# A column roll on one core: the head columns in sixteen stages through one pair of buffers instead of four stages with buffers of their own

## The chip, the cores and the metric

The kernel runs on one core of one Trainium2 chip. Time is device time in microseconds of one execution of the whole program; a kernel's time is the median over its runs. The profile is of one such execution, and "span" is the time from its first to its last profiled instruction.

## The reference

```python
x = np.random.randn(8192, 8192).astype(np.float32)
shift = 100

def reference(x, shift):
    return np.roll(x, shift, axis=1)
```

Every row of 8192 floats is turned to the right by 100 places: `out[r, c] = x[r, c - 100]`, and the last 100 columns of a row come to its front. There is no arithmetic; 268 MB are read and 268 MB written.

## The kernel before

The kernel cuts each row in two. With `s = 100` the cut column is `a = 256`, and `g = a - s = 156`.

**The bulk** is columns 256 to 8191 of the output, copied from HBM to HBM (line 43). Rows are taken in 128 blocks of 64; a block is four DMAs of 16 rows each, in turn on SP's and on ACT's queue. A row of a DMA is 31,744 B, one DMA 496 KB. In the last four blocks each is cut into two of half the width. Nothing waits for the bulk and it waits for nothing.

**The heads** are columns 0 to 255 of the output, 1 KB a row, and go through SBUF on GpSimd's queue. Four consecutive rows are numbered `q = 0..3`. For rows `q = 1..3` one read (`t`, line 73) fetches 256 floats that begin 100 floats ahead of the row: these are the last 100 of the row before and the first 156 of the row itself. So `t[q - 1]` holds the front part of output row `q - 1` (its first 100 columns) and the back part of output row `q` (its other 156). Two small reads complete the set: the last 100 floats of row 3 (line 74) and the first 156 of row 0 (line 77), straight into `h`. Two copies on DVE (lines 75 and 78) put the halves from `t` into `h`, whose rows are then the finished heads, and four stores (line 82), one for each `q`, write them.

Before the change a stage is 2048 rows: 128 partitions, `J = 4` groups of four rows in each, so that a large read and a store carry 512 rows of 1 KB. There are four stages, and each has buffers of its own (`bufs=n_st`). The first loop (lines 67 to 79) issues all the reads and copies of all stages, the second loop (lines 80 to 82) all the stores.

What orders this work: GpSimd issues its DMAs one after another, in the order of the program. The framework gives these DMAs eight completion semaphores in rotation, so a DMA can't be issued before the one eight places ahead of it has landed. It also writes the waits that the data need: a copy for the reads it uses, a store for the copies and small reads that filled its rows, and, where a buffer is used again, the new writer for the last reader.

Of the kernel before, what the change touches and what calls it, by code (L numbers as in the profile page):

```python
# [1 line left out]

# [4 lines left out]


@with_exitstack
def kernel(  # L10
    ctx: ExitStack,
    tc: tile.TileContext,
    x: bass.AP,
    shift: int,
    out: bass.AP,
):
    nc = tc.nc
    n_rows, n_cols = x.shape
    s = shift % n_cols
    a = -(-s // 128) * 128  # L20
    if 0 < a <= 384 and a + 128 <= n_cols:
        a += 128
    g = a - s
    P = nc.NUM_PARTITIONS
    engines = [nc.sync, nc.scalar]
    n_chunks = 16
    rows = n_rows // n_chunks

    xm = x.rearrange("(c e j) w -> c j e w", e=16, j=4)
    om = out.rearrange("(c e j) w -> c j e w", e=16, j=4)
    if a < n_cols:
        blocks = n_rows // 64
        mid = (a + n_cols) // 256 * 128
        for c in range(blocks):
            parts = ((a, mid), (mid, n_cols)) if c >= blocks - 4 and a < mid else ((a, n_cols),)  # L40
            for j in range(4):
                for lo, hi in parts:
                    engines[j % 2].dma_start(out=om[c, j, :, lo:hi], in_=xm[c, j, :, lo - s:hi - s])
    if a == 0:
        return


    if a > 512:
        for i in range(n_chunks):
            r = slice(i * rows, (i + 1) * rows)  # L50
            nc.gpsimd.dma_start(out=out[r, :s], in_=x[r, n_cols - s:])
            if g > 0:
                nc.gpsimd.dma_start(out=out[r, s:a], in_=x[r, :g])
        return

    Q, J = 4, 4  # L60
    n_st = n_rows // (P * Q * J)
    reads = ctx.enter_context(tc.tile_pool(name="reads", bufs=n_st))
    heads = ctx.enter_context(tc.tile_pool(name="heads", bufs=n_st))
    xt = x.rearrange("(k p j q) c -> k q p j c", q=Q, j=J, p=P)
    ot = out.rearrange("(k p j q) c -> k q p j c", q=Q, j=J, p=P)
    tiles = []
    for k in range(n_st):
        t = reads.tile([P, Q - 1, J, a], x.dtype)
        h = heads.tile([P, Q, J, a], x.dtype)
        for q in range(1, Q):  # L70
            lead = bass.AP(tensor=x.tensor, offset=(k * P * J * Q + q) * n_cols - s,
                           ap=[[J * Q * n_cols, P], [Q * n_cols, J], [1, a]])
            nc.gpsimd.dma_start(out=t[:, q - 1], in_=lead)  # L73
        nc.gpsimd.dma_start(out=h[:, Q - 1, :, :s], in_=xt[k, Q - 1, :, :, n_cols - s:])  # L74
        nc.vector.tensor_copy(h[:, :Q - 1, :, :s], t[:, :, :, :s])  # L75
        if g > 0:
            nc.gpsimd.dma_start(out=h[:, 0, :, s:], in_=xt[k, 0, :, :, :g])  # L77
            nc.vector.tensor_copy(h[:, 1:, :, s:], t[:, :, :, s:])  # L78
        tiles.append(h)
    for k, h in enumerate(tiles):  # L80
        for q in range(Q):
            nc.gpsimd.dma_start(out=ot[k, q, :, :, :a], in_=h[:, q])  # L82


# [1 line left out]
_INS = ['x', 'shift']  # L86
_OUTS = [((8192, 8192), 'float32')]

_NUMBERS = {'shift': 100}


# [26 lines left out]
```

## Time and profile before

| | us |
|---|---|
| four runs | 833.5, 830.17, 828.19, 826.13 |
| median | 829.18 |
| the profiled execution | 833.5 |
| its span | 831.3 |
| DVE busy | 7.7 (8 copies) |
| POOL busy | 28.8 (40 instructions, 36 of them DMA issues) |
| first and last bulk issue | 0.7 and 824.6 |
| first and last head store issued | 183.9 and 379.2 |

How to read it: SP and ACT only issue DMAs here, and issuing is not counted as busy on them. On POOL, DMA_DIRECT2D is the issue of a DMA. The queue q0 is GpSimd's (the heads), q1 and q10 are SP's and ACT's (the bulk). The row "GB/s" gives, in 40 equal slices of the span (20.8 us each), what the DMA engines moved; a byte copied from HBM to HBM counts once there, although it is read from HBM and written to it. DVE's two copies of a stage take 0.79 us (line 75) and 1.1 to 1.3 us (line 78). The median times from issue to landing are 12.8 us for a bulk DMA of 496 KB, 5.9 to 6.0 us for those of 248 KB at the end, 97.2 us for a large head read, 95.2 and 100.3 us for the small ones, and 115.7 us for a head store.

### The profile page before, as it was taken

What the parts mean: (1) busy time and instruction counts of PE and PEld (TensorE: products, weight loads), DVE (VectorE), ACT (ScalarE), POOL (GpSimd) and SP (SyncE); (2) the same over time, 40 slices, a digit from 0 to 9 for tenths busy, and PEclk for the clock granted to TensorE, in tenths of its full rate; (3) what the DMA queues carried; (4) which work ended last, traced back from release to release, by engine and by line L of the source; (5) the groups of instructions that cost most, each with busy time, mean ns of one, the idle gap of its engine ahead of it and who ended that gap; (6) DMA issues with size and microseconds to landing.
All of it is one profiled execution on the core that took longest, in us unless ns stands there. A gap on an engine that the chain in (4) does not pass through costs nothing. (4 is left out here: it accounts for less than half of the span.)

```text
span 831.3 us, 633 instructions
## 1 busy us (share of the span) xinstructions
DVE 7.7 (1%) x8; POOL 28.8 (3%) x40
## 2 busy tenths in 40 slices
DVE  0000000000000000000000000000000000000000
POOL 3000000010010000000000000000000000000000
DMA  9999999999999999999999999999999999999998
GB/s 300 340 335 338 341 352 339 342 342 353 350 335 347 344 344 354 344 350 339 339 326 323 328 321 331 319 335 325 322 341 319 330 333 325 327 333 322 333 306 295
DMA packets 21572, 276.89 MB, mean 333 GB/s; under 512 B 9024, under 2 KB 9024, under 8 KB 13120
## 3 DMA queue, kind: packets, MB, share of 16 engines
q10 hardware_dynamic: 8448, 130.04, 46.5%
q1 hardware_dynamic: 8448, 130.04, 46.0%
q0 software_dynamic: 4672, 16.78, 6.6%
q14 instruction: 4, 0.03, 0.0%
HBM read 268.44 MB, written 268.44 MB: 646 GB/s over the span
## 5 line engine op out<-in xcount | busy, mean ns | idle before, releaser
L82 POOL DMA_DIRECT2D out_dram<-h x16 | 13.2, 825 | 199.5 <-DMA out_dram<-h 112.0
L73 POOL DMA_DIRECT2D t<-in_x_dram x12 | 9.5, 793 | 61.3 <-DMA h<-in_x_dram 32.1
L75 DVE COPY h<-t 128x1200 f32<-128x1200 f32 x4 | 3.1, 785 | 239.1 <-DMA t<-in_x_dram 239.1
L78 DVE COPY h<-t 128x1872 f32<-128x1872 f32 x4 | 4.9, 1225 | 0.0
L74 POOL DMA_DIRECT2D h<-in_x_dram x4 | 3.0, 747 | 46.0 <-DMA t<-in_x_dram 46.0
L77 POOL DMA_DIRECT2D h<-in_x_dram x4 | 3.0, 748 | 44.0 <-DMA t<-in_x_dram 44.0
L99 POOL MEMSET const-float32-0.0<- 128x1 f32 x1 | 0.1, 98 | 0.2 <-issue 0.2
L99 POOL MEMSET const-bfloat16-1.0<- 128x1 bf16 x1 | 0.1, 101 | 0.0
L99 POOL MEMSET const-uint8-127<- 128x1 uint8 x1 | 0.1, 100 | 0.0
L99 POOL MEMSET const-float32-1.0<- 128x1 f32 x1 | 0.1, 98 | 0.0
## 6 DMA issues: line engine op xcount, KB each, us to landing
out_dram<-in_x_dram SPq DMA_DIRECT2D x248, 496.0 KB, 12.8
out_dram<-in_x_dram ACTq DMA_DIRECT2D x248, 496.0 KB, 12.8
out_dram<-h POOLq DMA_DIRECT2D x16, 512.0 KB, 115.7
t<-in_x_dram POOLq DMA_DIRECT2D x12, 512.0 KB, 97.2
out_dram<-in_x_dram SPq DMA_DIRECT2D x16, 248.0 KB, 5.9
out_dram<-in_x_dram ACTq DMA_DIRECT2D x16, 248.0 KB, 6.0
h<-in_x_dram POOLq DMA_DIRECT2D x4, 312.0 KB, 95.2
h<-in_x_dram POOLq DMA_DIRECT2D x4, 200.0 KB, 100.3
```

The source lines that it names most:

```text
L73: nc.gpsimd.dma_start(out=t[:, q - 1], in_=lead)
L74: nc.gpsimd.dma_start(out=h[:, Q - 1, :, :s], in_=xt[k, Q - 1, :, :, n_cols - s:])
L75: nc.vector.tensor_copy(h[:, :Q - 1, :, :s], t[:, :, :, :s])
L77: nc.gpsimd.dma_start(out=h[:, 0, :, s:], in_=xt[k, 0, :, :, :g])
L78: nc.vector.tensor_copy(h[:, 1:, :, s:], t[:, :, :, s:])
L82: nc.gpsimd.dma_start(out=ot[k, q, :, :, :a], in_=h[:, q])
L99: nc = _bacc.Bacc("TRN2", target_bir_lowering=False, num_devices=1)
```

## The change

A stage is now 512 rows: one group of four rows in each partition, so that a large read and a store carry 128 rows of 1 KB. There are sixteen stages. Both pools have one buffer, so every stage uses the same `t` and the same `h`. The second loop is gone: a stage's four stores are issued right behind its reads and copies. The bulk is not touched.

```diff
-    Q, J = 4, 4
-    n_st = n_rows // (P * Q * J)
-    reads = ctx.enter_context(tc.tile_pool(name="reads", bufs=n_st))
-    heads = ctx.enter_context(tc.tile_pool(name="heads", bufs=n_st))
-    xt = x.rearrange("(k p j q) c -> k q p j c", q=Q, j=J, p=P)
-    ot = out.rearrange("(k p j q) c -> k q p j c", q=Q, j=J, p=P)
+    Q = 4
+    n_st = n_rows // (P * Q)
+    reads = ctx.enter_context(tc.tile_pool(name="reads", bufs=1))
+    heads = ctx.enter_context(tc.tile_pool(name="heads", bufs=1))
+    xt = x.rearrange("(k p q) c -> k p q c", q=Q, p=P)
+    ot = out.rearrange("(k p q) c -> k p q c", q=Q, p=P)
     tiles = []
     for k in range(n_st):
-        t = reads.tile([P, Q - 1, J, a], x.dtype)
-        h = heads.tile([P, Q, J, a], x.dtype)
+        t = reads.tile([P, Q - 1, a], x.dtype)
+        h = heads.tile([P, Q, a], x.dtype)
         for q in range(1, Q):
-            lead = bass.AP(tensor=x.tensor, offset=(k * P * J * Q + q) * n_cols - s,
-                           ap=[[J * Q * n_cols, P], [Q * n_cols, J], [1, a]])
+            lead = bass.AP(tensor=x.tensor, offset=(k * P * Q + q) * n_cols - s, ap=[[Q * n_cols, P], [1, a]])
             nc.gpsimd.dma_start(out=t[:, q - 1], in_=lead)
-        nc.gpsimd.dma_start(out=h[:, Q - 1, :, :s], in_=xt[k, Q - 1, :, :, n_cols - s:])
-        nc.vector.tensor_copy(h[:, :Q - 1, :, :s], t[:, :, :, :s])
+        nc.gpsimd.dma_start(out=h[:, Q - 1, :s], in_=xt[k, :, Q - 1, n_cols - s:])
+        nc.vector.tensor_copy(h[:, :Q - 1, :s], t[:, :, :s])
         if g > 0:
-            nc.gpsimd.dma_start(out=h[:, 0, :, s:], in_=xt[k, 0, :, :, :g])
-            nc.vector.tensor_copy(h[:, 1:, :, s:], t[:, :, :, s:])
-        tiles.append(h)
-    for k, h in enumerate(tiles):
+            nc.gpsimd.dma_start(out=h[:, 0, s:], in_=xt[k, :, 0, :g])
+            nc.vector.tensor_copy(h[:, 1:, s:], t[:, :, s:])
         for q in range(Q):
-            nc.gpsimd.dma_start(out=ot[k, q, :, :, :a], in_=h[:, q])
+            nc.gpsimd.dma_start(out=ot[k, :, q, :a], in_=h[:, q])
```

## The prediction

> **What bounds the kernel now.** I read the page from its slices down, then the timeline of GpSimd's queue, then the table by windows. The page first:
>
> ```profile
> DMA  9999999999999999999999999999999999999998
> GB/s 300 340 335 338 341 352 339 342 342 353 350 335 347 344 344 354 344 350 339 339 326 323 328 321 331 319 335 325 322 341 319 330 333 325 327 333 322 333 306 295
> DMA packets 21572, 276.89 MB, mean 333 GB/s; under 512 B 9024, under 2 KB 9024, under 8 KB 13120
> q10 hardware_dynamic: 8448, 130.04, 46.5%
> q1 hardware_dynamic: 8448, 130.04, 46.0%
> q0 software_dynamic: 4672, 16.78, 6.6%
> HBM read 268.44 MB, written 268.44 MB: 646 GB/s over the span
> ```
>
> The DMA engines are busy in every slice; DVE and POOL are busy for 7.7 and 28.8 us of 831.3. The end is set by the bulk on SP's and ACT's queues (q1, q10), whose last transfers are issued at 824.6 us. Heads (q0) are 16.78 of 276.89 MB. So the question is not what the head path costs, but when it ends, and what a byte costs.
>
> The issues of GpSimd's queue give the pace (start, duration, instruction, and in brackets the idle time before it and what ended it):
>
> ```profile
> 62.40 0.75 POOL L73 DMA_DIRECT2D t<-in_x_dram  x1 [5.54 <-DMA h<-in_x_dram]
> ...
> 125.30 0.75 POOL L73 DMA_DIRECT2D t<-in_x_dram  x1 [6.34 <-DMA h<-in_x_dram]
> ...
> 261.45 0.71 POOL L82 DMA_DIRECT2D out_dram<-h  x1 [8.19 <-DMA h<-in_x_dram]
> ...
> 379.16 0.71 POOL L82 DMA_DIRECT2D out_dram<-h  x1 [12.55 <-DMA out_dram<-h]
> ```
>
> Each issue waits for the landing of the DMA eight places earlier. Eight stores take (379.16 - 261.45) / 8 = 14.7 us each; a stage of five reads takes 125.30 - 62.40 = 62.9 us. The last store is issued at 379.2 and lands some 116 us later (the median of its row in the issues), at 495: heads are done 335 us before the bulk.
>
> **What a packet costs.** There are 528 + 36 = 564 DMAs, and 564 x 16 = 9024 is exactly the count under 512 B: every DMA closes with one signal on each of 16 engines. On q0 that leaves 4672 - 576 = 4096 data packets of 4096 B on average for 36 x 512 = 18,432 rows: the short rows go out packed, some 4.5 to a packet, and none is under 2 KB. A 512 KB DMA is then 8 data packets and a signal per engine, 9 turns: 14.7 / 9 = 1.63 us a turn. During the stores a 512 KB DMA every 14.7 us is 35.7 GB/s; the window 320 to 400 us moves 346, so the bulk moves 310, or 19.4 GB/s per engine, and in 1.63 us that is 31.7 KB: one bulk packet (496 KB over 16 engines is 31,744 B). So a head packet waits for one bulk packet, and a signal takes a turn like any other. The reads: 3 x 9 turns, and for the two small ones 8 data packets and 2 signals, 37 turns in 62.9 us, 1.70 us each.
>
> **The byte price.** Two lines of the table by windows (window, length, busy, clock, DMA share, GB/s) stand for storing and bulk alone:
>
> ```profile
> 320.00:400.00 80.00, 0.00 (x0) 3.57 (x5) 1.00 1.01 346
> 520.00:600.00 80.00, 0.00 (x0) 0.00 (x0) 1.00 1.00 326
> ```
>
> Bulk bytes touch HBM twice, head bytes once. Storing: 2 x 310 + 36 = 656 GB/s of HBM; bulk alone 652, and 660 in the window 680 to 760 (330 GB/s). While heads are read (80 to 160 us, 341 GB/s) a stage of 2.10 MB in 62.9 us is 33 GB/s, so 2 x 308 + 33 = 649. HBM traffic is what is nearly constant; a head byte costs its share whenever it is moved.
>
> **The change, part by part.**
>
> *Bytes and rows:* the same; no term.
>
> *DMAs:* 144 instead of 36, each of 128 rows. Issue takes POOL 0.75 us for 512 rows, so 108 more are at most 81 us, between about 0 and 0.75 each; I take the upper end. Per stage that is 9 x 0.75 = 6.8 us, and it lies beside packets in flight. There are 108 more signals per engine; a signal's record in the trace takes 9 ns, so 1 us of engine time, but each costs the head queue a turn.
>
> *Turns per stage:* three reads of 8 KB per engine, 2 data and a signal, 9 turns; the small reads of 3.2 and 5.0 KB per engine, 2 and 3 turns, 5 together; four stores, 12. At the prices above 14 x 1.70 + 12 x 1.63 = 43.4 us a stage, 694 us for 16. The first DMA of the run landed some 9 us later than its turns say (about 24 us instead of 15), so heads end near **705 us**, against 495, and still 125 us before the bulk.
>
> *New waits:* with one pair of buffers, in the built program's waits, (a) the two small reads of a stage wait for the four stores of the stage before; queued behind them on POOL are only the stores, and the three large reads have been issued ahead, 9 turns or 15 us of queued work. (b) The copies on DVE wait for the large reads and those stores, and the first stores for the copies: at most 2.1 us of copies (0.79 + 1.32 before, for four times the size) and 1.6 us for an issue behind them, under 5 turns (8.5 us) of small reads. (c) The last two stores (three in the first stage) wait for the small reads, under 6 turns of the first two stores, 9.8 us. Each handover has a cover longer than its cost, so I take 0 a stage; without covers I bound it at 3 x 4 = 12 us (copies and issue of 3.7 us at (b) taken for all three).
>
> *Old waits removed:* the eight-deep run-ahead. The trace's 16 signals of the store issued at 307.3 us arrive from 317.6 to 423.0: most engines are soon done, four lag by up to 72 turns. Now no engine can be more than about a stage ahead. The slow ones set the pace in both forms, and I count nothing.
>
> *Interleaving:* reads at 649 instead of 656 GB/s for 180 us cost 2 us now; spread over 700 us this may vanish or double. I put -4 to +5 us on it, with the start, and take +1 for the signals.
>
> **The sum** on the profiled execution: 833.5 us (span 831.3) + 0 + 1 = 834.5. That execution was the slowest of four; carried to the median 829.18, the forecast is **830 us**. A step of 1% either way, 8 us, is about what a measurement of this kernel can tell from no change.
>
> **A rule against it.** The Trainium skill, "Trainium Kernel Development and Optimization", Best Practices, asks for double buffering so that DMA and compute overlap; one pair of buffers breaks that, and whether the queue's cover replaces it no run shows yet. The skill's "DMA: Bandwidth & Descriptors", Anatomy of one DMA, gives a GpSimd DMA a fixed cost of about 2.0 us; by it, as an estimate, 108 more DMAs paid one after another would be 216 us, and heads would end near 711 us, which is no other time for the kernel. The trace's price of a signal turn, 1.63 us, is near that figure.
>
> **The rivals.**
>
> *Heads outlast the bulk (slower).* The place is the three handovers, and it decides from (826 - 10) / 16 = 51 us a stage, 7.6 us above my sum. For it: every handover waits for the slowest of 16 engines, and the engines scatter by tens of us today. Against: the covers. At 43.4 + 12 = 55 us a stage, 14.9 stages are done when the bulk ends near 828 us; the other 1.1 run alone. No row shows a lone stage; the nearest is the last bulk transfers, landing 5.9 us after issue, so three legs are 18 us, between 3 us (1 MB at 333 GB/s) and the full 55. 1.1 x 18 = 20 us: 848 us on the profiled scale, **844** on the median. Chance 0.24.
>
> *The rows are no longer packed.* If a packet held one row, a large DMA would be 9 turns, a stage 81, some 135 us; 6 stages would be done at the bulk's end, and ten at 25 us would follow: about **1060 us**. Against it: the 400 B and 624 B rows, too, went packed, since no data packet is under 2 KB. Chance 0.03.
>
> *Bulk and heads disturb each other.* Heads now pass 512 rows in 43 us where the bulk takes 52, so both work on nearly the same rows throughout; today heads ran far ahead. If the 649 GB/s of the reading phase held to 705 us instead of 180, 1.1% of 525 us, 6 us, would be lost, and above 1% with the start: **838**. Chance 0.05.
>
> *Faster.* If mixing restored 656 GB/s throughout and smoothed the start (318 GB/s in the first 40 us), 4 us would go: **825**. That is inside 1% and part of my forecast; beyond it no row has a price. A gain over 1%, 815 to 820, keeps 0.06 for engines that lag less when heads cannot pile up eight deep.
>
> **How the numbers follow.** Heads stay hidden: 0.62, with a range of its own of 823 to 836. Slower by over 1% is 0.24 + 0.03 + 0.05 = 0.32, faster 0.06. The range reaches from 822, just inside the gain, to 850, over the 844 of the first rival, and leaves out the unpacked case, part of the gain and the worse end of the handovers.
>
> **What would show it.** In the slices GB/s should lie near 335 to 345 up to about slice 34 and fall to 328 after, where now the step is at slice 20. The last head store should be issued near 685 us; stores of successive stages should be 43 us apart; the landing of a large read should fall from 97 us to 20 to 35 us. q0 should hold some 6,400 to 6,700 packets. HBM should stay at 645 GB/s. I am wrong if stages are over 51 us apart, if q0 has packets under 2 KB by the thousand, or if the bulk's own issues end later than 830 us while the heads are long done.

## The result

The changed kernel takes 831.16 us in the median of 50 runs, the kernel before 829.54 us in 79: a ratio of 1.0019, with a 95% interval of 1.0012 to 1.0026. That is 1.6 us, 0.2%, clear of the noise but within the 1% that was called no change. The forecast was 830, with a range of 822 to 850.

The profiled execution took 831.86 us (span 830.1). The same lines of its page as those shown of before:

```profile
DMA  9999999999999999999999999999999999999998
GB/s 305 346 328 332 335 346 336 343 333 337 335 340 337 338 337 346 345 333 342 342 330 343 336 342 331 336 339 339 342 337 341 334 328 320 332 327 330 321 306 295
DMA packets 23559, 276.92 MB, mean 334 GB/s; under 512 B 10752, under 2 KB 11008, under 8 KB 15104
q1 hardware_dynamic: 8448, 130.04, 45.8%
q10 hardware_dynamic: 8448, 130.04, 44.2%
q0 software_dynamic: 6656, 16.79, 8.9%
HBM read 268.44 MB, written 268.44 MB: 647 GB/s over the span
```

The DMA engines are as full as before, and HBM carries 647 GB/s over the span against 646. What has moved is the step in the row GB/s: the heads' share now lies over slices 1 to 32 of 40, where it lay over the first 20 to 24. Heads end at 673 us (the last packet of q0 in the trace) instead of 495, still 156 us before the last packet of the bulk.

The queues' shares say more. The heads' packets now take 8.9% of the time of the 16 DMA engines, where they took 6.6%, and the bulk's take 90.0% where they took 92.5%. A bulk packet of 31,744 B passed in 1448 ns on average, against 1492 in the kernel before. So the longer time of the heads on the engines did not add to the time of the kernel: the bulk's packets became shorter by about as much, which fits a limit that lies in the traffic and not in the engines' time.

The timeline of GpSimd's queue shows one stage of the steady state and the last stores (start, duration, instruction, and in brackets the idle time before it and what ended it):

```profile
615.02 1.60 POOL L72 DMA_DIRECT2D t<-in_x_dram  x3
630.78 0.53 POOL L73 DMA_DIRECT2D h<-in_x_dram  x1 [14.16 <-DMA out_dram<-h]
631.31 0.54 POOL L76 DMA_DIRECT2D h<-in_x_dram  x1
647.28 1.08 POOL L79 DMA_DIRECT2D out_dram<-h  x2 [15.43 <-DVE h L77]
653.29 1.07 POOL L79 DMA_DIRECT2D out_dram<-h  x2 [4.93 <-DMA h<-in_x_dram]
```

The three handovers can be read from the brackets: the small reads wait for the stores, the first two stores for the copies, the last two for the small reads. The copies on DVE give the spacing of stages (line 74, the second stage and the last):

```profile
67.95 0.37 DVE L74 COPY h<-t 128x300 f32<-128x300 f32 x1 [47.25 <-DMA t<-in_x_dram]
...
646.24 0.37 DVE L74 COPY h<-t 128x300 f32<-128x300 f32 x1 [39.61 <-DMA t<-in_x_dram]
```

(646.24 - 67.95) / 14 = 41.3 us a stage, where 43.4 was forecast and 51 was the limit. The table by windows, with heads under way and with the bulk alone:

```profile
320.00:400.00 80.00, 0.75 (x2) 8.52 (x16) 1.00 1.00 341
...
680.00:760.00 80.00, 0.00 (x0) 0.00 (x0) 1.00 0.99 325
```

A stage moves 1.05 MB of heads in 41.3 us, 25 GB/s, so the first window has 2 x 316 + 25 = 657 GB/s of HBM traffic and the second 2 x 325 = 650. The 649 GB/s that the prediction read beside the head reads did not become the rule for the whole time of the heads, which its third rival had allowed for.

One trap lies in the page's chain that ended last. It runs here through `t`, `h` and the stores, 61% DMA, as if the heads set the end. It is followed back from the last instruction, and no instruction waits for the bulk, so the bulk isn't in it. The slices and the last packets of the queues show what ends last.

### The profile page after: what moved, and what is told of

Read it like the earlier page. It is cut to its first block, busy times and chain, and to the rows that moved or that the text cites. A ratio compares the mean times of both kernels' runs of the same rounds, so it can differ in the third digit from the quotient of the medians.

```text
span 830.1 us, 875 instructions
## 1 busy us (share of the span) xinstructions
DVE 12.0 (1%) x32; POOL 77.2 (9%) x148
## 3 DMA queue, kind: packets, MB, share of 16 engines
q0 software_dynamic: 6656, 16.79, 8.9%
## 4 chain that ended last, share of the span: by engine, by line
DMA 61%; issue 11%; POOL 5%; DVE 1%; DVEq 0%; POOLq 0%; PEldq 0%
DMA t<-in_x_dram 37%; DMA h<-in_x_dram 13%; DMA out_dram<-h 11%; POOL out_dram L79 3%; POOL t L72 1%; DVE h L77 1%; DVE h L74 1%; POOL h L73 0%; DVEq L74 0%; POOLq L110 0%; DVEq L110 0%; POOLq L79 0%; POOLq L73 0%; PEldq L110 0%; POOLq L72 0%
## 5 line engine op out<-in xcount | busy, mean ns | idle before, releaser
L79 POOL DMA_DIRECT2D out_dram<-h x64 | 34.4, 542 | 342.5 <-DVE h L77 230.2
L73 POOL DMA_DIRECT2D h<-in_x_dram x16 | 8.5, 534 | 233.5 <-DMA out_dram<-h 233.5
L72 POOL DMA_DIRECT2D t<-in_x_dram x48 | 25.7, 542 | 0.8 <-PEq L110 0.8
L74 DVE COPY h<-t 128x300 f32<-128x300 f32 x16 | 5.9, 367 | 635.0 <-DMA t<-in_x_dram 475.6
L76 POOL DMA_DIRECT2D h<-in_x_dram x16 | 8.6, 536 | 0.0
L77 DVE COPY h<-t 128x468 f32<-128x468 f32 x16 | 7.5, 468 | 0.0
## 6 DMA issues: line engine op xcount, KB each, us to landing
out_dram<-in_x_dram SPq DMA_DIRECT2D x248, 496.0 KB, 12.8
out_dram<-in_x_dram ACTq DMA_DIRECT2D x248, 496.0 KB, 12.8
out_dram<-h POOLq DMA_DIRECT2D x64, 128.0 KB, 14.6
t<-in_x_dram POOLq DMA_DIRECT2D x48, 128.0 KB, 25.8
```

The costliest lines, as they stand in the source:

```text
L73: nc.gpsimd.dma_start(out=h[:, Q - 1, :s], in_=xt[k, :, Q - 1, n_cols - s:])
L74: nc.vector.tensor_copy(h[:, :Q - 1, :s], t[:, :, :s])
L76: nc.gpsimd.dma_start(out=h[:, 0, s:], in_=xt[k, :, 0, :g])
L77: nc.vector.tensor_copy(h[:, 1:, s:], t[:, :, s:])
L79: nc.gpsimd.dma_start(out=ot[k, :, q, :a], in_=h[:, q])
```

## The experiments

The theory on trial: heads are hidden, the bulk and the HBM traffic set the time, and only heads that end later than the bulk cost anything beyond their bytes. Its rivals: that handovers cost the bulk something, and that heads cost by turns.

**The bulk alone.** A `return` ahead of line 44; the heads are left out.

```diff
+    return
     if a == 0:
         return
```

> Leaves out the heads: columns 0 to 255 of the output are not written. What do the heads cost the bulk when they are hidden? Theory (heads are hidden and cost their share of HBM traffic): 16.78 MB at the 656 GB/s of HBM traffic that the windows of the kernel before give is 25.6 us, so 829.5 - 25.6 = 804 us. Rival (the slow engines alternate one head packet or signal with one bulk packet, so that heads cost by turns): 292 turns at 1.63 us against bulk packets at 1.54 us alone is 0.09 us a turn, 26 us before, and 416 turns would make 37 us after; then the bulk alone is again near 804, but the changed kernel would be 11 us slower than before, which it is not. A third reading, that heads go into gaps and cost nothing, gives 829.

Measured: 800.3 us, a ratio of 0.9644 (0.9617 to 0.9672). The heads cost 29.5 us on that chip, not 25.6, and certainly not nothing: a head that ends 335 us early is paid for in full. Bulk packets of 31,744 B pass in 1534 ns on average here, more slowly than beside heads (1492 and 1448), so the heads don't cost the time that they spend on the engines. By turns the changed kernel would have had to be 11 us slower than before; it is 1.6.

**The heads alone.** The bulk is left out.

```diff
-        blocks = n_rows // 64
+        blocks = 0
```

> Leaves out the bulk: only columns 0 to 255 are written, by the changed kernel's sixteen stages. It prices a stage without the bulk. The prediction took 18 us a stage from the last bulk transfers (three legs of 5.9 us): 16 x 18 + 12 = 300 us. If the page's fixed cost and the packets alone counted it would be nearer the lower bound of 3 us a stage, some 60 us.

Measured: 124.5 us. First and last copy on line 74 start at 5.09 and 115.52 us, so a stage takes 110.43 / 15 = 7.4 us. The issues (KB each, and the median from issue to landing) show why, first of this kernel, then of the changed one:

```profile
out_dram<-h POOLq DMA_DIRECT2D x64, 128.0 KB, 2.1
t<-in_x_dram POOLq DMA_DIRECT2D x48, 128.0 KB, 2.6
```

```profile
out_dram<-h POOLq DMA_DIRECT2D x64, 128.0 KB, 14.6
t<-in_x_dram POOLq DMA_DIRECT2D x48, 128.0 KB, 25.8
```

The same transfers, with the same bytes, land in 2.1 and 2.6 us without the bulk and in 14.6 and 25.8 us beside it. The 41.3 us of a stage are waiting for turns, and so little else that a stage without the bulk needs less than a fifth. The 18 us of the prediction, taken from bulk transfers that still had company, was 2.4 times too high.

**One tile for `t` and `h`.** The large reads now wait for the stores as well.

```diff
-        t = reads.tile([P, Q - 1, a], x.dtype)
-        h = heads.tile([P, Q, a], x.dtype)
+        th = heads.tile([P, 2 * Q - 1, a], x.dtype)
+        t, h = th[:, :Q - 1], th[:, Q - 1:]
```

> One buffer for t and h together, so that the large reads too wait for the four stores of the stage before: cover (a), the 9 turns of reads issued ahead, is taken away. Theory (only the end of the heads counts, and a bare handover costs an issue, a first packet and a landing, 4 to 8 us): stages 45 to 50 us apart instead of 41.3, heads end at 720 to 800 us, time within 0.4% of the changed kernel, 829 to 834 us. Rival (the bulk pays for handovers, since engines stand still on the head queue): the 0.2% of the change grows with the bare handover, to 0.5% or more, 835 us. If stages rise above 51 us, heads end last and the time is above 840.

Measured: 830.62 us, a ratio of 1.0011 (0.9994 to 1.0028). The copies in its timeline, second and last stage:

```profile
69.89 0.37 DVE L73 COPY th<-th 128x300 f32<-128x300 f32 x1 [48.68 <-DMA th<-in_x_dram]
766.92 0.37 DVE L73 COPY th<-th 128x300 f32<-128x300 f32 x1 [46.71 <-DMA th<-in_x_dram]
```

A stage takes 697.03 / 14 = 49.8 us and the heads end at 792 us, 35 us ahead of the bulk. Without its cover the handover costs 8.5 us, so cover (a) of the prediction did what was said of it. And 119 us of delay at the end of the heads cost the kernel nothing that 10 runs can tell: the heads stay hidden even when they end this close to the bulk.

**Thirty-two stages of 256 rows.**

```diff
-    Q = 4
+    Q, P = 4, P // 2
```

> Thirty-two stages of 256 rows (64 partitions): 18 turns a stage at 1.59 us (41.3 us for 26 turns in the changed kernel) is 28.6 us, 916 us for all, so the heads must outlast the bulk. Theory: the bulk ends near 825 us, 28.6 stages are done, and the other 3.4 run alone at a price between 3 and 18 us a stage: 835 to 890 us, 860 with 10 us. q0 should hold 32 x 18 x 16 = 9,216 packets. If the time stays within 1% of 830, a turn is not what a stage costs, and heads of small stages are faster than turns say.

Measured: 849.34 us, a ratio of 1.0242 (1.0206 to 1.0277); the profiled execution was the longest of the four, 853.22. q0 holds 9,216 packets. Copies of the second, the 27th and the last two of 32 stages:

```profile
48.66 0.36 DVE L74 COPY h<-t 64x300 f32<-64x300 f32 x1 [32.86 <-DMA h<-in_x_dram]
...
780.45 0.36 DVE L74 COPY h<-t 64x300 f32<-64x300 f32 x1 [28.76 <-DMA t<-in_x_dram]
...
837.18 0.36 DVE L74 COPY h<-t 64x300 f32<-64x300 f32 x1 [5.62 <-DMA t<-in_x_dram]
843.71 0.36 DVE L74 COPY h<-t 64x300 f32<-64x300 f32 x1 [5.78 <-DMA t<-in_x_dram]
```

Stages are 29.3 us apart (731.79 / 25) while the bulk runs and 6.5 us apart once it is done. The bulk's last packet ends at 827.7 us, the heads' at 847.9. Of all the kernels with a bulk, only here the heads are the end; its page shows it as a last slice of 65 GB/s:

```profile
GB/s 312 332 335 334 329 328 336 332 336 332 338 336 338 319 333 335 336 336 336 337 338 327 333 336 336 331 335 340 331 330 336 350 334 329 334 347 325 293 312 65
```

So what the first rival said of the end is right: heads outlast the bulk when their stages are too slow, and the kernel is then late by the stages left over, at the price of a stage alone. What made these stages slow is not its handovers, though, but the turns: 18 of them were expected to take 28.6 us.

**The change again, and its halves.** On another chip, with 11 or 12 runs each: the changed kernel; sixteen stages of 512 rows with buffers of their own and all reads first; four stages of 2048 rows in turn through one pair. The second of these against the changed kernel:

```diff
-    reads = ctx.enter_context(tc.tile_pool(name="reads", bufs=1))
-    heads = ctx.enter_context(tc.tile_pool(name="heads", bufs=1))
+    reads = ctx.enter_context(tc.tile_pool(name="reads", bufs=n_st))
+    heads = ctx.enter_context(tc.tile_pool(name="heads", bufs=n_st))
...
+        tiles.append(h)
+    for k, h in enumerate(tiles):
         for q in range(Q):
```

The third against the kernel before:

```diff
-    reads = ctx.enter_context(tc.tile_pool(name="reads", bufs=n_st))
-    heads = ctx.enter_context(tc.tile_pool(name="heads", bufs=n_st))
+    reads = ctx.enter_context(tc.tile_pool(name="reads", bufs=1))
+    heads = ctx.enter_context(tc.tile_pool(name="heads", bufs=1))
...
-        tiles.append(h)
-    for k, h in enumerate(tiles):
         for q in range(Q):
```

> The changed kernel itself, beside the two that make half of the change each. Expected 831.2 against 829.5 us before, a ratio of 1.002, with stages 41 us apart.

> Only the size: sixteen stages of 512 rows, but every stage with buffers of its own and all reads ahead of all stores, as before. 416 turns at 1.63 us: heads end near 680 us, held by the eight semaphores alone. If the 1.6 us of the change come from the number of DMAs and signals (288 against 72 a pair of loops would be more, 144 against 36 here), this kernel is at 1.002 too. If they come from the order (reads and stores in turn, one pair of buffers), it is at 1.000.

> Only the order: four stages of 2048 rows, one pair of buffers, each read and stored in turn. A stage is 37 read turns at 1.70 and 36 store turns at 1.63, 122 us, heads end near 495 us. By the order theory the ratio is 1.002, by the theory of DMAs and signals 1.000. In both the time stays within 0.5% of before, since heads end 330 us before the bulk.

| kernel | us | ratio to before (95%) | heads end, us |
|---|---|---|---|
| before | 827.76 | 1 | 495 (its profile above) |
| changed | 829.11 | 1.0021 (1.0010 to 1.0031) | 679 |
| sixteen stages, reads first | 828.09 | 1.0003 (0.9991 to 1.0015) | 675 |
| four stages in turn | 827.88 | 0.9997 (0.9986 to 1.0008) | 490 |

(A ratio here is worked out from all the runs with its interval; it can differ in the fourth decimal from the quotient of the two medians.)

The third row tests the handovers: without a single one of the new waits, the same 144 DMAs end at 675 us, where the changed kernel's heads end at 673 to 679 in its three profiles. The new waits cost the heads no more than the old ones did. This kernel isn't free of waits, however: its queue still waits 55 times for an earlier store, 229.8 us in all, because of the eight semaphores. The two pairs of buffers below put a number on the handover itself. In the same way the four stages in turn end at 490 us, where they ended at 495 with all reads first.

The kernel with sixteen stages and reads first also gives the price of a turn. The first and the last of its 64 stores:

```profile
341.69 0.55 POOL L81 DMA_DIRECT2D out_dram<-h  x1 [5.02 <-DVE h L74]
639.40 0.54 POOL L81 DMA_DIRECT2D out_dram<-h  x1 [3.63 <-DMA out_dram<-h]
```

They are issued 4.73 us apart, for two data packets and a signal; before, eight data packets and a signal took 14.71 us. If all data turns cost the same, and all signals' turns, the two rates give 1.66 us for a data turn and 1.40 for a signal's. This is an estimate, but the reads give nearly the same for the signal: a stage of 9 data turns and 5 signals takes 22.7 us here (its copies on line 74 go from 22.09 to 316.91 us in 13 stages), one of 32 and 5 took 62.9 before, and that is 1.75 us and 1.39.

Neither half alone is slower by a measurable amount, and neither theory of the 0.2% is confirmed.

**Reads only.** The kernel before without its stores (the loop in lines 80 to 82); columns 0 to 255 of the output stay unwritten.

```diff
-    for k, h in enumerate(tiles):
-        for q in range(Q):
-            nc.gpsimd.dma_start(out=ot[k, q, :, :, :a], in_=h[:, q])
```

> The kernel before without the head stores: columns 0 to 255 of the output are not written. It splits the 29.5 us that heads cost (829.8 - 800.3) between reads and stores. By bytes alone 8.39 MB at 656 GB/s is 12.8 us, 813.1 us. With HBM at 649 GB/s while heads are read (1.1% of 250 us) it is 815.9, so that reads cost 15.6 us and stores 13.9. If reads and stores cost the same it is 815.0; the two theories are hardly apart, but above 818 or below 812 both are wrong.

Measured: 814.62 us, a ratio of 0.9840 (0.9822 to 0.9858). The bulk alone stood at 0.9644 on the other chip, so the reads cost 0.0196 of the time, 16.3 us, and the stores the other 13.2. By bytes alone each would be 12.8. The intervals leave the split uncertain by some 4 us, so it isn't shown that reads cost more than stores.

**What makes the 0.2%.** A last set on one chip, 12 runs each: the changed kernel once more; its stages in reverse order; two pairs of buffers; the one tile again. The edits of the second and third, against the changed kernel:

```diff
-    for k in range(n_st):
+    for k in reversed(range(n_st)):
```

```diff
-    reads = ctx.enter_context(tc.tile_pool(name="reads", bufs=1))
-    heads = ctx.enter_context(tc.tile_pool(name="heads", bufs=1))
+    reads = ctx.enter_context(tc.tile_pool(name="reads", bufs=2))
+    heads = ctx.enter_context(tc.tile_pool(name="heads", bufs=2))
```

> The changed kernel once more, as the measure for the next three: 1.002 of before.

> The changed kernel with its stages from the last rows to the first, so that heads are at the bulk's rows only once, in the middle of the run. Neither half of the change alone gave the 0.2%. Theory of place (heads pass 512 rows in 41 us, the bulk in 52, both begin at row 0, and work on near rows disturbs): 1.000. Theory of mixture (small reads and stores in turn for 670 us, wherever they are): 1.002. The end of the heads near 675 us in both.

> The changed kernel with two pairs of buffers, so that the small reads wait for the stores of two stages before. If the waits of the single pair make the 0.2%, 1.000; if the order alone does, 1.002. The pace is set by turns either way: stages 41 us apart, heads end near 675 us; if handovers had cost time after all, the stages come nearer together, 38 us or less.

> One buffer for both again, now in five rounds: stages 49.8 us apart, heads end at 792 us. If the excess grew with the time that heads are under way (672 us in the changed kernel), 1.0025; if it belongs to the waits, more than 1.002; by the theory of place, since 49.8 us is nearly the bulk's 52, the most of all kernels, 1.004.

| kernel | us | ratio to before (95%) | heads end, us |
|---|---|---|---|
| before | 828.18 | 1 | |
| changed | 829.07 | 1.0011 (0.9998 to 1.0024) | 675 |
| stages reversed | 828.95 | 1.0006 (0.9993 to 1.0020) | 669 |
| two pairs | 828.91 | 1.0009 (0.9999 to 1.0020) | 656 |
| one tile | 828.73 | 1.0014 (1.0000 to 1.0028) | 801 |

All four lie between 1.0006 and 1.0014, and no two can be told apart. The theory of place asked for 1.004 of the one tile, which lies outside its interval. The reversed stages, for which it asked 1.000, decide nothing, since the changed kernel itself stands at only 1.0011 in this set.

With two pairs the stages come in twos, so their spacing is read from one stage to another of the same pair of buffers (line 74, the first two stages and the last two):

```profile
20.47 0.37 DVE L74 COPY h<-t 128x300 f32<-128x300 f32 x1 [20.47 <-DMA t<-in_x_dram]
45.42 0.37 DVE L74 COPY h<-t 128x300 f32<-128x300 f32 x1 [24.20 <-DMA t<-in_x_dram]
...
590.03 0.37 DVE L74 COPY h<-t 128x300 f32<-128x300 f32 x1 [55.79 <-DMA t<-in_x_dram]
613.48 0.37 DVE L74 COPY h<-t 128x300 f32<-128x300 f32 x1 [22.69 <-DMA h<-in_x_dram]
```

That is (590.03 - 20.47) / 14 = 40.7 us a stage, and 40.6 for the other pair. The changed kernel's stages were 41.3 us apart, and 41.9 in its profile of this set ((650.01 - 64.10) / 14). So a handover takes about 1 us of a stage, less than the 3 us that would have spoken against the covers. The heads end 19 us earlier with two pairs mostly because of the start: the second stage's copy runs at 45.42 us instead of 64.10. What makes the 0.2% stays open.

## Why the prediction was right

**What bounds the kernel** held: the bulk is the end, the HBM traffic is nearly constant (650 to 657 GB/s in the windows above), and the change moves no byte more or less. The bulk alone, the one tile and the thirty-two stages show from three sides that only the end of the heads and their bytes count. That HBM itself sets the limit is read from this constancy; no run tests it by itself.

**What a packet costs** was right on average and not in its mechanism: "a head packet waits for one bulk packet". The trace's packets can be sorted by engine, since nearly every packet begins within 10 ns of the end of another. While the kernel before stores (262 to 490 us), what lies between two head packets of an engine is exactly two of the bulk's signals in 39% of cases, exactly two of its data packets in 37%, and nothing in 16%. The engines mostly take one packet from each of the three queues in turn, and since every second packet of the bulk is a signal, a head packet waits for two of the bulk's data packets one time and for none the next, one on average.

**Turns per stage** was the step that decided, and it was right in its count: q0 holds 6,656 packets, the count for 2 + 1 turns in a large DMA and 1 + 1 and 2 + 1 in the small reads. Its price was a little high: 43.4 us a stage against 41.3, and 705 us for the end against 673 to 679. The term that was mis-sized is the signal. It was priced like a data packet, at 1.63 us or 1.70, and the estimate from the rates of stores is 1.40 against 1.66 for data; 17 data turns and 9 signals are then 40.8 us. The first stage was not late by the 9 us allowed, either: its first copy started at 20 us.

**New waits, each with a cover.** That they cost about 0 was right to within about 1 us a stage, by the two pairs of buffers. In the stage shown above the reads issued ahead at 615.0 to 616.6 us still end the wait of DVE at 646.24, 15.5 us after the stores have landed: the queue of waiting reads covers the handover with 9 turns, as worked out. Covers (b) and (c) are seen there too. By the trace's signals the small reads land at 649.6 and 653.0 us, after the first two stores have been issued at 647.28, and those land at 659.8 and 663.3, after the last two have been issued at 653.29. The one tile put a price of 8.5 us on that handover once it is bare, above the 4 to 8 expected; the 12 us a stage taken as the end without any cover was not tried.

**The byte price** was too low: 29.5 us measured (27 to 32 by its interval) against the 25.6 that 656 GB/s gives. It doesn't enter the forecast, since both kernels move the same bytes.

**Interleaving** was allowed -4 to +5 us, and the sum took +1 us for the signals alone. The whole change measured +0.9 to +1.6 in its three sets, so the agreement with the +1 is luck: the sixteen stages with reads first have the same signals and stand 0.3 us above before. Where the 0.2% comes from was not found.

**The rival of the handovers** had its limit right and its price wrong. At 49.8 us heads were hidden, and at 29.3 us for half a stage, 58.6 for 512 rows, they were not. But the late part runs at 7.4 us a stage, not 18, so 55 us a stage would have cost, as an estimate, about 1.1 x 7.4 = 8 us and not 20.

**The two rules** that spoke against the change: double buffering (the Trainium skill, "Trainium Kernel Development and Optimization", Best Practices) was not needed here, since a second pair brought the heads' end from 675 to 656 us and the kernel nothing. The fixed cost of about 2.0 us for a DMA ("DMA: Bandwidth & Descriptors", Anatomy of one DMA) agrees with the heads alone, where a store of 128 KB lands after 2.1 us in all; beside the bulk the same store takes 14.6, so there the queue counts and not the fixed cost.

## What to carry to other kernels

Ask of a side stream first when it ends and what ends last, and price its stages in turns of the queue beside the main stream, not in bytes or in latency alone: 512 KB took 14.7 us there, and 128 KB not a quarter of it, but 4.7. A handover on a queue cost next to nothing here (about 1 us of 41) as long as something issued ahead was still waiting in that queue, and 8.5 us once nothing was; count that queue in turns, and find out at what stage time the cover ends. Small buffers are then free to within 0.2%, up to a limit that can be worked out beforehand: here the end of the bulk divided by the number of stages.

## What had not been expected

A stage of heads takes 7.4 us alone and 41.3 us beside the bulk, although the heads are 6% of the bytes. A signal without data waits about 1.40 us for its turn, nearly as long as 4 KB: what either waits for is the bulk's packets. The engines scatter far apart under long queues: 105 us between the first and the last of the 16 signals of one store in the kernel before, when eight DMAs could pile up, and 9 us for the last store of the changed kernel, whose stages hold them together (664.2 to 673.4 us). Over all stores the medians are 103 and 8 us. That neither helped the bulk nor, beyond the 0.2%, hurt it.
